# Two attention heads of a pair issued as one interleaved group of half-array matmuls

## The chip, the core and the metric

The kernel runs on one core of a Trainium2 chip. The core has a matrix engine (TensorE, PE in the profile, with its weight loads as a row of their own, PEld), a vector engine (VectorE, DVE), a scalar engine (ScalarE, ACT), GpSimd (POOL) and SyncE (SP), whose queue issues all DMA transfers here. Each engine runs its own list of instructions in order, and they meet at semaphores. TensorE multiplies a stationary operand, loaded into an array of 128 by 128 cells, with a moving operand that streams through it, and writes its sums into eight banks of PSUM. A product with only 64 contraction rows occupies one half of the rows of the array, a product with only 64 stationary columns one half of its columns.

The metric is the device time of one execution in microseconds, as the median of several runs.

## The reference

The reference is two transformer blocks over 256 tokens of width 1024, all in float32. Block 1 has two attentions side by side (latent attention and block attention), and a mixture of 32 experts. Block 2 has an even layer (a gated convolution beside differential attention) and an odd layer (stick-breaking attention), each followed by attention to 256 memory tokens and a gated feed-forward part. Cut to what matters here:

```python
# latent attention: 8 heads, queries and keys 96 wide, values 64 wide
s = jnp.einsum('bqhd,bkhd->bhqk', qi, k) * scale
p = jax.nn.softmax(jnp.where(kpos[None, :] <= qpos[:, None], s, -jnp.inf))
o = jnp.einsum('bhqk,bkhd->bqhd', p, v)
# block attention: 8 heads, all 64 wide; with 256 tokens there is one block, so it is causal attention
# even mixer: 4 pairs of heads, queries and keys 64 wide, values 128 wide
p = probs(q1, k1) - lam * probs(q2, k2);  o = einsum(p, v)
# odd mixer: 16 heads, all 64 wide
z = jnp.einsum('bhqd,bhkd->bhqk', qb, k) * scale
a = exp(log_sigmoid(z) + sum over later keys of log_sigmoid(-z)), keys before the query only
o = jnp.einsum('bhqk,bhkd->bhqd', a, v)
```

## The kernel before

All weights come from memory in slabs of 1 MB. A slab is split into two parts, h on ACT and l on DVE (`slab`, line 539), so that a product with float32 accuracy is made of three products in a faster format, f32r. The helper `fm` (line 658) multiplies a slab with the activations, features by tokens, and `tm` (line 671) tokens by features. Attention itself, the transposes and the statistics are plain float32 matmuls; the profile shows each of those as two passes.

The network is not issued as it is written. Each operation is recorded with the tiles that it reads and writes (`record`, line 223); then a list scheduler (`plan`, line 290) simulates the five engines with a price for each operation (`price`, line 191) and picks an order: on each engine the ready operation that was recorded first goes first, and where none of an earlier phase is ready, one of a later phase does. What is recorded in one call of `record` stays together on its engine; separate calls can come apart. An operation that starts a tile waits for a free place of its tag: `bank` (line 476) gives three banks of PSUM to products with weights, two each to the chains `a` and `b`, to which the pairs of heads go in turn, and one to the rest. The price of a float32 matmul is halved where it uses at most 64 rows or columns. All instructions are issued from line 461, so the profile knows them by their tiles.

Each pair of heads is a chain. In the block attention (`block1_attention`, lines 876 to 892) queries and keys of two heads are transposed together, one head in partitions 0 to 63 and the other in 64 to 127 (tile `qt`). `scores_causal` (line 707) then makes the scores of one head in a bank of its own (`sc`): a 128 by 128 product for the first half of the queries, and a 128 by 256 product for the second half. The mask is added by a bf16 product, DVE takes the maximum (`nm`), ACT the exponential (`p`), and the probabilities are transposed on TensorE and copied to `pt`. `pair_out` (line 917) multiplies them with the values, by `pv` (line 749): two matmuls for each head, 256 and 128 columns, into one half of the partitions of the bank `bo`. When both heads are in, ACT and DVE split the result into `xh` and `xl`.

The latent attention (lines 855 to 869) treats its heads one by one, as they are 96 wide, and uses `pair_out` as well. The even mixer (lines 1352 to 1391) uses `scores_causal` for the two heads of each pair on the tile `eqk`; its value product is 128 wide and is a call of `pv` of its own. The odd mixer (lines 1437 to 1477) makes transposed scores `oz` for both heads of `oqk` in a loop (lines 1450 to 1456), turns them into `op` through `oe`, `oeh` and `oel`, with further products into the same bank, and ends in `pair_out`.

So there are 16 pairs whose scores are 64 rows high (4 in the block attention, 4 in the even mixer, 8 in the odd mixer), and 16 pairs whose values are 64 columns wide (4 in the latent attention, 4 in the block attention, 8 in the odd mixer).

Of the kernel before, what the change touches and what calls it, by code (L numbers as in the profile page):

```python
# [17 lines left out]
PSUM = bass.MemoryType.PSUM  # L18
# [45 lines left out]
# Each engine runs its instructions in the order in which they are issued. The  # L64
# network is first recorded, phase after phase, on tiles that have no place yet;
# a list scheduler then picks the order, so that an engine that would wait for
# one phase works on the next. Tile places the tiles and makes all waits.
class View:
    """A part of a recorded tile."""
# [54 lines left out]
class Slot:  # L124
    """A recorded tile."""
# [38 lines left out]
class Recorder:  # L164
# [18 lines left out]
    def stray(self, shape, dtype, name):  # L183
        """A tile that takes a place that any of the tags in self.shared can spare."""
        return Slot(self, shape, dtype, name, None, 0, "sb").view()
# [97 lines left out]
    def barrier(self, fn, views):  # L283
        """All that was recorded before comes before fn(), all that follows after it, except loads."""
        self.bars.append((len(self.ops), fn, [v.tile for v in views]))
        for v in views:
            v.tile.ops.add(("bar", len(self.bars)))

# [1 line left out]
    def plan(self):  # L290
        """An order of everything recorded: on each engine the ready operation of the lowest prio goes first."""
# [17 lines left out]
        def spare(op):  # L309
            """The shared tag that can best spare a place for op: those of earlier ops stay."""  # L310
            best = None
            for tag in self.shared:
                n = len(free[tag]) - max(0, bisect.bisect_left(self.starts[tag], op.idx) - turn[tag])
                if n > 0 and (best is None or n > best[0]):
                    best = n, tag
            return best and best[1]
# [5 lines left out]
        def load():  # L322
            """Start the loads in the order of the program, as far as there are places."""
            nonlocal due
            while due < len(loads):
                op = loads[due]
                t = op.allocs[0]
                if t.tag is None:
                    tag = spare(op)
                    if tag is None:  # L330
                        return
                    take(op, t, tag)
                elif t.seq == turn[t.tag] and free[t.tag]:
                    take(op, t, t.tag)
                    turn[t.tag] += 1
                else:
                    return
                due += 1
                push(op)
# [4 lines left out]
        def offer(op):  # L344
            """Hand a free place to each tile that op starts, in the order of the program, if there are."""
# [88 lines left out]
    def run(self):  # L434
# [7 lines left out]
        # a table is loaded as soon as the one before has done its last  # L442
# [21 lines left out]
class Net:  # L464
# [11 lines left out]
    def bank(self, tag, name):  # L476
        """A bank of PSUM: g for products with weights, a and b for chains in turn, m for the rest."""
        return self.rec.tile([128, 512], F32, name, "p" + tag, dict(g=3, a=2, b=2, m=1)[tag], "ps")

    def temp(self, p, name, shape, dt=F32):  # L480
        """A short-lived tile of chain p, or of the norms (p = "s")."""
        return self.rec.tile(shape, dt, name, "t" + p, 2 if p == "s" else NT)
# [50 lines left out]
    def raw(self, ap):  # L533
        """A slab of weights as it is."""
        w = self.rec.stray([128, WMAX], F32, "w")
        self.rec.sync.dma_start(w, ap)
        return w

    def slab(self, ap, inner, before=None):
        """A slab of weights in two parts that add up to it exactly, each [128, n / inner, inner].  # L540
        With before, it comes in four pieces, and before(i) comes before piece i."""
# [18 lines left out]
    def mm3(self, todo):  # L560
        """out += s.T @ m, with s = sh + sl and m = mh + ml, for each of todo."""
# [7 lines left out]

    def mm(self, out, lhs, rhs, start=True, stop=True):  # L570
        self.rec.tensor.matmul(out, lhs, rhs, start=start, stop=stop, skip_group_check=True)
# [4 lines left out]
    def parts(self, hi, lo, src, gain=None):  # L576
        """hi + lo = src (times the gain of each partition)."""
# [20 lines left out]
    def rsq(self, p, out, ms, n, mul=1.0):  # L598
        """out = mul / sqrt(ms + EPS), n columns"""
# [11 lines left out]
    def mean(self, acc):  # L611
        """From the sum of squares [128, 2 x 256]: the mean square of each token, on every partition."""
        b = self.bank("m", "st")
        self.rec.vector.tensor_tensor(acc[:, :T], acc[:, :T], acc[:, T:], ALU.add)
        self.mm(b[:, :T], self.k1024, acc[:, :T])
        return b[:, :T]
# [30 lines left out]
    def norm_parts(self, src, gain, stats=True):  # L647
        """Parts of src times gain, and the sum of squares of src."""
# [9 lines left out]
    def fm(self, w, x, kcs=None, cols=0, name="fm", tag="g"):  # L658
        """Two chunks of 128 output features by 256 tokens."""
# [13 lines left out]
    def tm(self, b, w, x, kcs, t, cols, first=True, last=True):  # L673
        """128 tokens by the given columns."""
# [22 lines left out]
    def project(self, w, m):  # L697
        """x += m @ w"""
# [6 lines left out]
    HALVES = ((0, slice(0, 128)), (1, slice(128, 384)))  # L705

    def scores_causal(self, p, q, k):
        """q, k: [d, 256]; scores of both query tiles in one bank: 128 columns of query tile 0, then
        256 of query tile 1."""
# [9 lines left out]
    def softmax_causal(self, p, b, scale=1.0):  # L719
        """exp(scale * (scores - max)) and one over the sums."""  # L720
# [13 lines left out]
    def attend(self, p, b):  # L734
        """Transposed probabilities: key tile 0 by 256 queries, key tile 1 by the last 128."""
# [36 lines left out]
    def block1_attention(self, steps):  # L772
        nc, a = self.rec, self.a
        x, _ = self.norm_parts(self.x, "attn_norm", False)
        # latents of the queries and of the keys and values
# [28 lines left out]
        # by token: rotary key, block attention's queries, keys, values  # L804
# [29 lines left out]
        # latent attention: queries, keys, values by token  # L834
# [41 lines left out]
        for i in range(4):  # L876
            p = "ab"[i % 2]
            bt = self.bank(p, "qkt")
            for n in range(2):
                for t in range(2):  # L880
# [5 lines left out]
            bs = [self.scores_causal(p, qt[64 * j:64 * j + 64, 0:256], qt[64 * j:64 * j + 64, 256:512])  # L886
                  for j in range(2)]
# [5 lines left out]
        # gates  # L893
# [23 lines left out]
    def pair_out(self, p, pts, v, i, ox, c):  # L917
        """Outputs of two heads, from their transposed probabilities."""
        bo = self.bank(p, "bo")
        for j in range(2):  # L920
            hv = slice(128 * i + 64 * j, 128 * i + 64 * j + 64)
            self.pv(bo[64 * j:64 * j + 64, :], v[:, 0, hv], v[:, 1, hv], pts[j])
        self.parts(ox[0][:, c, :], ox[1][:, c, :], bo[:, :T])

# [1 line left out]
    def first_of(self, out, values, best, shape):  # L926
        """One-hot of the first place where values == best."""
# [8 lines left out]
    def route(self, rtm):  # L936
        """Weights and places in line of every token at every expert."""
# [49 lines left out]
        # weights  # L987
# [17 lines left out]
        # those that come after an expert's first SLOTS  # L1005
# [10 lines left out]
    def moe(self, steps, early, every):  # L1016
        nc, a, x = self.rec, self.a, self.x
        # tokens, neither normalised nor times the gain, by token
# [104 lines left out]
    def moe_late(self, hh, hl, rtm, wlate, flag):  # L1123
        """The tokens that come after an expert's first SLOTS, whenever there are any."""
# [64 lines left out]
    def two_norms(self):  # L1189
        """The final norm of block 1 and the first of block 2: parts of x times both gains, and the factor  # L1190
        that normalises their products by token. x becomes the normalised output of block 1."""
# [30 lines left out]
    def head_norm(self, p, b, ones, pairs, rbc, out, gains, mul=1.0):  # L1222
        """Normalise the rows of a bank [128, 2 x 256] by head: over both halves together (pairs)
        or within each (not pairs); out [128, 2, 256]."""
# [18 lines left out]
    def memory(self):  # L1243
        """Keys and values of the memory tokens for both layers, as a list of steps."""
# [84 lines left out]
    def even_mixer(self, x, rbc):  # L1329
# [3 lines left out]
        # lambda  # L1333
# [9 lines left out]
        # distance bias of each head, times 8, with the mask of the last 128 columns  # L1343
# [8 lines left out]
        for hd in range(4):  # L1352
# [10 lines left out]
            bs = []  # L1363
            for m in range(2):
                r = slice(64 * m, 64 * m + 64)
                bs.append(self.scores_causal(p, qk[r, 0, :], qk[r, 1, :]))
# [16 lines left out]
            # sub-layer norm, times 1 - lambda_init  # L1383
# [8 lines left out]
        # gated convolution  # L1392
# [26 lines left out]
    def conv(self, o, u, w):  # L1419
        """Causal convolution of width 3 along the tokens; u has two zero columns in front."""  # L1420
# [5 lines left out]
    def odd_mixer(self):  # L1426
# [10 lines left out]
        for i in range(8):  # L1437
# [12 lines left out]
            bz = []  # L1450
            for j in range(2):
                r = slice(64 * j, 64 * j + 64)
                b = self.bank(p, "oz")
                self.mm(b[:, 0:T], k[r, 0:128], q[r, :], True, False)
                self.mm(b[:, T:384], k[r, 128:T], q[r, 128:T], False, False)
                bz.append(b)
# [106 lines left out]
def layouts(i):  # L1563
    """The inputs as the kernel reads them: moved, never computed on."""
# [119 lines left out]
```

## Time and profile before

| what | value |
|---|---|
| median of 3 runs | 1302.47 us (1300.27 to 1303.06) |
| span of the profiled execution | 1302.4 us |
| TensorE busy | 1234.3 us, 95% |
| DVE busy | 852.8 us, 65% |
| ACT busy | 651.8 us, 50% |
| float32 value products of 64-wide heads (`bo<-pt,vs` and `bo<-op,ov`) | 64 + 64 passes, 28.2 us busy |
| scores of the odd mixer (`oz<-oqk`) | 64 passes, 11.1 us busy |
| scores of the even mixer (`sc<-eqk`) | 32 passes, 3.7 us busy |
| scores in block 1 (`sc<-qt`), latent heads among them | 64 passes, 11.0 us busy |
| DMA | 273.55 MB, mean 210 GB/s |

A row such as `PE MATMUL bo<-op,ov 128*64 128x256 f32 x4` reads: TensorE, operation, the tile written and the tiles read, rows and columns of the array that are used, partitions and elements of the moving operand, and how many such instructions. Matmuls are pipelined and their ends are modelled, so busy time counts overlapping instructions once and says little about what one costs; the distance from one start to the next says more.

### The profile page before, as it was taken

The page shows a single profiled execution, that of the slowest core. Times are in us where ns is not written, and L with a number is a line of the kernel's source. Part 1 is how long each engine was busy: PE and PEld are TensorE (multiplying, and loading weights), DVE is VectorE, ACT ScalarE, POOL GpSimd, SP SyncE. Part 2 cuts the span into 40 slices and gives each one's busy share as a digit, 9 for nine tenths or more (in the row PEclk, how much of TensorE's full clock was granted, in tenths as well). Part 3 has the DMA queues.
Part 4 walks back from the last instruction along what each step waited for, and adds up shares of the span by engine and source line. Part 5 has one row for each costly group of instructions (what it writes and reads, how often), then busy time and mean ns, then how long its engine had stood idle before and what let it go on. Part 6 is the DMA issues. An engine that isn't in the chain of part 4 may idle for free.

```text
span 1302.4 us, 22667 instructions
## 1 busy us (share of the span) xinstructions
PE 1234.3 (95%) x9325; PEld 1091.3 (84%) x9325; DVE 852.8 (65%) x1529; ACT 651.8 (50%) x1111; POOL 8.9 (1%) x71
## 2 busy tenths in 40 slices
PE   7999999987878876999999999999999999999998
PEld 7988999656545542898999999999998999999997
DVE  7666578524442242898877977777745587877775
ACT  6654455423322231664545655555656655555553
POOL 1000000000000000000000000000000000000000
PEclk9999999998989998999999999999999999999999
DMA  7623375798999989353441555555333251555551
GB/s 257 241 98 130 136 285 204 309 393 333 381 379 396 419 335 406 133 191 123 156 175 66 198 196 186 170 191 193 131 130 114 81 194 66 203 185 189 174 188 65
DMA packets 40143, 273.55 MB, mean 210 GB/s; under 512 B 4576, under 2 KB 4576, under 8 KB 8032
## 3 DMA queue, kind: packets, MB, share of 16 engines
q1 hardware_dynamic: 40032, 272.03, 56.1%
q8 instruction: 75, 1.23, 0.4%
q14 instruction: 36, 0.29, 0.1%
HBM read 270.96 MB, written 1.05 MB: 209 GB/s over the span
## 4 chain that ended last, share of the span: by engine, by line
PE 67%; DVE 4%; DMA 2%; ACT 2%; issue 1%; SPq 0%; DVEq 0%; ACTq 0%
PE fm L461 40%; PE dn L461 10%; PE tm L461 4%; PE gu L461 2%; PE co L461 2%; PE oz L461 2%; DMA w<-w_dn 2%; DVE l L461 2%; PE by L461 2%; PE bo L461 1%; PE mo L461 1%; PE ms L461 1%; PE ga L461 1%; PE hn L461 1%; DMA w<-w_gu 1%
## 5 line engine op out<-in xcount | busy, mean ns | idle before, releaser
L461 PE MATMUL fm<-xh,h 128*128 128x256 f32 x1824 | 529.0, 291 | 14.1 <-ACT h L461 6.6
L461 PE MATMUL fm<-xh,l 128*128 128x256 f32 x1824 | 520.1, 286 | 6.7 <-DVE l L461 6.7
L461 PE MATMUL fm<-xl,h 128*128 128x256 f32 x1824 | 518.5, 285 | 0.0
L461 DVE TENSOR_TENSOR l<-w,h 128x1024 fp32r<-128x1024 f32 (+2 forms) x328 | 383.1, 1191 | 59.9 <-ACT h L461 59.2
L461 ACT ACTIVATE h<-w 128x1024 fp32r<-128x1024 f32 (+2 forms) x328 | 325.4, 1027 | 176.3 <-issue 85.1
L461 PEld LDWEIGHTS fm<-xh,h 128*128 128x128 f32 x1824 | 352.0, 193 | 19.2 <-ACT h L461 7.4
L461 PEld LDWEIGHTS fm<-xh,l 128*128 128x128 f32 x1824 | 352.0, 193 | 8.3 <-DVE l L461 8.0
L461 PEld LDWEIGHTS fm<-xl,h 128*128 128x128 f32 x1824 | 352.4, 193 | 2.1 <-issue 0.7
L461 PE MATMUL tm<-l,xh 128*128 128x256 f32 (+2 forms) x364 | 104.5, 288 | 4.0 <-DVE l L461 4.0
L461 PE MATMUL tm<-h,xh 128*128 128x256 f32 (+2 forms) x364 | 107.2, 296 | 0.1
L461 PE MATMUL tm<-h,xl 128*128 128x256 f32 (+2 forms) x364 | 104.0, 286 | 0.0
L461 DVE SCALAR_TENSOR_TENSOR fc<-fu,partile,fc 128x256 f32<-128x256 f32 x176 | 73.5, 480 | 1.3 <-ACT fc L461 1.3
L461 PEld LDWEIGHTS tm<-l,xh 128*128 128x128 f32 x364 | 69.5, 191 | 5.2 <-DVE l L461 4.6
L461 PEld LDWEIGHTS tm<-h,xh 128*128 128x128 f32 x364 | 69.4, 191 | 3.3 <-issue 1.6
L461 PE MATMUL gu<-w,xs 128*32 128x512 f32 x512 | 65.6, 630 | 6.0 <-DMA w<-w_gu 6.0
L461 PEld LDWEIGHTS tm<-h,xl 128*128 128x128 f32 x364 | 69.5, 191 | 0.4
L461 PE MATMUL dn<-fa,h 128*128 128x256 f32 x352 | 64.2, 282 | 1.1 <-ACT fa L461 0.6
L461 DVE TENSOR_TENSOR x<-x,co 128x512 f32<-128x512 f32 x32 | 21.8, 687 | 57.9 <-PE co L461 57.9
L461 PE MATMUL dn<-h,fa 128*128 128x512 f32 x176 | 57.0, 396 | 0.0
L461 PEld LDWEIGHTS dn<-fa,h 128*128 128x128 f32 x352 | 54.4, 189 | 1.6 <-ACT fa L461 0.8
L461 DVE TENSOR_TENSOR fu<-fm,rbc 128x512 f32<-128x512 f32 x44 | 30.3, 688 | 37.9 <-PE fm L461 37.7
L461 DVE SCALAR_TENSOR_TENSOR act<-gu,rs,act 128x256 f32<-128x256 f32 x8 | 3.9, 484 | 71.8 <-ACT act L461 71.8
(291 smaller groups left out, 1416.1 us busy)
## 6 DMA issues: line engine op xcount, KB each, us to landing
w<-w_gu SPq DMA_DIRECT2D x64, 1024.0 KB, 9.3
w<-w_up SPq DMA_DIRECT2D x44, 1024.0 KB, 4.9
w<-w_dn SPq DMA_DIRECT2D x32, 1024.0 KB, 9.9
w<-w_down SPq DMA_DIRECT2D x22, 1024.0 KB, 4.9
w<-w_xkv SPq DMA_DIRECT2D x16, 1024.0 KB, 8.5
w<-w_in_d SPq DMA_DIRECT2D x8, 1024.0 KB, 4.8
w<-w_xq SPq DMA_DIRECT2D x8, 1024.0 KB, 4.9
w<-w_xo SPq DMA_DIRECT2D x8, 1024.0 KB, 5.1
```

Of the source, the lines that this page charges most:

```text
L461: getattr(getattr(self.nc, op.engine), method)(*map(r, a), **{n: r(v) for n, v in k.items()})
```

## The change

Three things become one recorded operation each, in which the two heads take turns: the scores of a pair in the block attention and in the even mixer (new function `scores_pair`), the scores of a pair in the odd mixer, and the value products of a pair in `pair_out`. A new helper `together` records a list of matmuls in one call. In the scores that come from `scores_pair` the 256-wide part now goes first and starts the bank. The latent attention's scores and the even mixer's value product are not touched. Comments and docstrings are gone too, as blank lines, so that most line numbers stay near their old places.

```diff
+    def together(self, *products):
+        self.rec.record("tensor", [("matmul", p[:3], dict(start=p[3], stop=p[4], skip_group_check=True))
+                                   for p in products])
...
+    def scores_pair(self, p, qs, ks):
+        bs = [self.bank(p, "sc") for _ in range(2)]
+        both = list(zip(bs, qs, ks))
+        self.together(*[(b[:, 128:384], q[:, 128:], k, True, False) for b, q, k in both],
+                      *[(b[:, :128], q[:, :128], k[:, :128], False, False) for b, q, k in both])
+        return bs
...
-            bs = [self.scores_causal(p, qt[64 * j:64 * j + 64, 0:256], qt[64 * j:64 * j + 64, 256:512])
-                  for j in range(2)]
+            bs = self.scores_pair(p, *([qt[64 * j:64 * j + 64, o:o + 256] for j in range(2)] for o in (0, 256)))
...
     def pair_out(self, p, pts, v, i, ox, c):
         bo = self.bank(p, "bo")
-        for j in range(2):
-            hv = slice(128 * i + 64 * j, 128 * i + 64 * j + 64)
-            self.pv(bo[64 * j:64 * j + 64, :], v[:, 0, hv], v[:, 1, hv], pts[j])
+        both = [(bo[64 * j:64 * j + 64, :], slice(128 * i + 64 * j, 128 * i + 64 * j + 64), pts[j]) for j in range(2)]
+        self.together(*[(o[:, :T], v[:, 0, hv], pt[:, :T], True, False) for o, hv, pt in both],
+                      *[(o[:, 128:T], v[:, 1, hv], pt[:, T:384], False, True) for o, hv, pt in both])
         self.parts(ox[0][:, c, :], ox[1][:, c, :], bo[:, :T])
...
-            bs = []
-            for m in range(2):
-                r = slice(64 * m, 64 * m + 64)
-                bs.append(self.scores_causal(p, qk[r, 0, :], qk[r, 1, :]))
+            bs = self.scores_pair(p, *([qk[64 * m:64 * m + 64, n, :] for m in range(2)] for n in range(2)))
...
-            bz = []
-            for j in range(2):
-                r = slice(64 * j, 64 * j + 64)
-                b = self.bank(p, "oz")
-                self.mm(b[:, 0:T], k[r, 0:128], q[r, :], True, False)
-                self.mm(b[:, T:384], k[r, 128:T], q[r, 128:T], False, False)
-                bz.append(b)
+            bz = [self.bank(p, "oz") for _ in range(2)]
+            both = [(b, slice(64 * j, 64 * j + 64)) for j, b in enumerate(bz)]
+            self.together(*[(b[:, 0:T], k[r, 0:128], q[r, :], True, False) for b, r in both],
+                          *[(b[:, T:384], k[r, 128:T], q[r, 128:T], False, False) for b, r in both])
```

## The prediction

> **What bounds the kernel now.** I read the page first, then a table of busy time by stretch, then the timeline of TensorE around single heads, and last the waits.
>
> ```profile
> PE 1234.3 (95%) x9325; PEld 1091.3 (84%) x9325; DVE 852.8 (65%) x1529; ACT 651.8 (50%) x1111; POOL 8.9 (1%) x71
> ...
> PE 67%; DVE 4%; DMA 2%; ACT 2%; issue 1%; SPq 0%; DVEq 0%; ACTq 0%
> ```
>
> TensorE is busy for 95% of the span and makes 67% of the chain that ended last. An average hides stages, so the next rows give the stretches that matter (columns: width, then busy time and count on each engine, clock, DMA share, GB/s).
>
> ```profile
> 60.00:112.00 52.00, 52.00 (x394) 45.98 (x394) 30.26 (x70) 28.41 (x68) 0.00 (x0) 1.00 0.34 118
> 112.00:147.00 35.00, 34.88 (x264) 28.83 (x263) 25.87 (x63) 18.91 (x48) 0.00 (x0) 1.00 0.28 97
> 147.00:244.00 97.00, 97.00 (x790) 93.83 (x789) 67.35 (x136) 48.07 (x66) 0.00 (x0) 1.00 0.64 236
> 244.00:520.00 276.00, 223.69 (x1621) 135.92 (x1619) 95.67 (x167) 79.94 (x116) 0.00 (x0) 0.95 0.95 381
> 555.00:625.00 70.00, 67.30 (x520) 62.58 (x519) 64.03 (x146) 38.78 (x81) 0.30 (x3) 0.98 0.43 151
> 915.00:1035.00 120.00, 119.42 (x903) 108.11 (x903) 63.23 (x95) 71.56 (x128) 0.00 (x0) 1.00 0.33 115
> ```
>
> The change touches the latent attention (60 to 112 us), the block attention (112 to 147), the even mixer (555 to 625) and the odd mixer (915 to 1035). In the first two and in the last TensorE has no idle time to speak of, because the planner fills every wait of the attention chains with weight products (`fm`, `tm`). There, time taken from TensorE should be time taken from the kernel. The expert stage between (244 to 520) hangs on DMA, share 0.95.
>
> **What a head's value product costs.** Busy time will not do for this, since matmuls overlap; starts do. The rows are start, length, engine, operation and merged count; a float32 matmul shows as two passes, so one head's two matmuls are x4.
>
> ```profile
> 931.63 0.28 PE L461 MATMUL fm<-xh,l 128*128 128x256 f32 x1
> 931.84 0.87 PE L461 MATMUL bo<-op,ov 128*64 128x256 f32 x4
> 932.64 0.39 PE L461 MATMUL fm<-xh,h 128*128 128x256 f32 x1
> 932.86 0.28 PE L461 MATMUL fm<-xl,h 128*128 128x256 f32 x1
> 932.98 0.28 PE L461 MATMUL fm<-xh,l 128*128 128x256 f32 x1
> ```
>
> In a steady run of `fm` a pass starts every 0.12 us (932.86 to 932.98). From the last `fm` at 931.63 to the second one after the group, at 932.86, 1.23 us pass where two steps would take 0.24: a head standing alone takes 0.99 us of TensorE. Of this 0.80 is the group itself (931.84 to 932.64) and 0.19 the slower entry (0.21 against 0.12) and return (0.22 against 0.12). How many there are:
>
> ```profile
> L461 PE MATMUL bo<-pt,vs 128*64 128x256 f32 (+1 forms) x64 | 14.4, 341 | 0.1
> L461 PE MATMUL bo<-op,ov 128*64 128x256 f32 (+1 forms) x64 | 13.8, 339 | 0.0
> ```
>
> 128 passes are 32 heads, 16 in block 1 and 16 in the odd mixer. The even mixer's value product is 128 wide and stays as it is. In the timeline no two heads' value products stand next to each other, for each is issued when its own probabilities are ready.
>
> **What two heads together cost.** The 64-wide value products exist nowhere side by side in this trace, so their price is bounded. One bound is scores, where two heads use the two row halves:
>
> ```profile
> 924.29 0.93 PE L461 MATMUL oz<-oqk 64*128 64x256 f32 x8
> 925.15 0.40 PE L461 MATMUL oz<-bf 128*128 128x128 bf16 x4
> ...
> 933.54 0.92 PE L461 MATMUL oz<-oqk 64*128 64x256 f32 x4
> 934.39 0.44 PE L461 MATMUL oz<-oeh,ntri 128*128 128x384 f32 x1
> 934.76 0.92 PE L461 MATMUL oz<-oqk 64*128 64x256 f32 x4
> 935.61 0.40 PE L461 MATMUL oz<-bf 128*128 128x128 bf16 x4
> ```
>
> Eight passes of two neighbouring heads take 0.86 us to the next operation, four passes of one head 0.85: the second head costs 0.01 us if it is next in the queue. This also says that adjacency alone is enough here, since the code before records all of one head and then all of the other. The interleaved order itself should be worth nothing. The other near row is the expert product, 32 columns wide, four column parts at once:
>
> ```profile
> 393.81 7.07 PE L461 MATMUL gu<-w,xs 128*32 128x512 f32 x64
> ...
> 394.27 0.13 PEld L461 LDWEIGHTS gu<-w,xs 128*32 128x32 f32 x4 [0.30 <-issue]
> ```
>
> 64 passes of 512 columns in 7.07 us are 0.11 us a pass, 0.22 ns a column; a lone head streams 768 columns in 0.80 us, 1.04 ns a column. So column parts run side by side as well, and four of their weight loads fit in 0.13 us. The other bound is no overlap at all: the second head then adds its whole 0.80. I take 0.01, the value of the row case, because the column row shows the same kind of overlap in the very direction that is asked of here.
>
> So a pair of value products goes from 2 x 0.99 to 1.00, and saves 0.97 us; 16 pairs save **15.6 us**. With no overlap it would be 0.19 a pair, 3.0 us.
>
> **What the scores save.** Where both heads already stand together nothing is left to gain: all four pairs of the even mixer (one is quoted), three of four in the block attention and two of eight in the odd mixer.
>
> ```profile
> 561.17 0.93 PE L461 MATMUL sc<-eqk 64*128 64x128 f32 x8
> 562.03 0.50 PE L461 MATMUL sc<-ali,bf 128*128 128x128 bf16 x4
> ```
>
> ```profile
> 126.08 0.92 PE L461 MATMUL sc<-qt 64*128 64x128 f32 x4
> 129.04 0.92 PE L461 MATMUL sc<-qt 64*128 64x128 f32 x4
> ```
>
> ```profile
> 958.75 0.92 PE L461 MATMUL oz<-oqk 64*128 64x256 f32 x6
> 959.60 0.86 PE L461 MATMUL bo<-op,ov 128*64 128x256 f32 x4
> 960.39 0.48 PE L461 MATMUL oz<-oqk 64*128 64x128 f32 x2
> 960.81 0.40 PE L461 MATMUL oz<-bf 128*128 128x128 bf16 x4
> ```
>
> ```profile
> 975.24 0.70 PE L461 MATMUL oz<-oqk 64*128 64x256 f32 x2
> 975.86 0.44 PE L461 MATMUL oz<-oel,ntri 128*128 128x384 f32 x1
> 976.45 0.92 PE L461 MATMUL oz<-oqk 64*128 64x128 f32 x6
> 977.31 0.40 PE L461 MATMUL oz<-bf 128*128 128x128 bf16 x4
> ```
>
> The pair at 126.08 and 129.04, and that at 933.54 and 934.76, are fully apart: about 0.97 each (0.85 and a switch). The kind at 958.75, three times in the odd mixer, takes 0.85 + 0.42 against 0.86 together and saves 0.41 and half a switch, 0.5 each. The kind at 975.24, twice, takes 0.62 + 0.86 against 0.86 and saves 0.62 and half a switch, 0.7 each. Together 1.0 in block 1 and 1.0 + 1.5 + 1.4 = 3.9 in the odd mixer, **4.9 us**. Starting the bank with the 256-wide part instead of the 128-wide one costs nothing: 924.29 and 561.17 have the two orders, and both take 0.86.
>
> **What is added and moved.** No DMA, no copy and no instruction is new. The first head's value product is moved behind the second head's probabilities. The group then waits for both on TensorE, and behind it in that queue stand the `fm` passes of the next slab, for whose banks DVE waits. But the second head's product waits for the same thing today, and that has cost almost nothing:
>
> ```profile
> PE bo L461 <- DVE pt L461: 0.3, 1, 0.3
> ```
>
> The output bank is evacuated when the second head is done, in both versions. Scores must now find two free banks of their chain at once; in the even mixer they find them at every pair, so I cost this at nothing. The cover is the stock of `fm` passes; what it costs without it is the third rival.
>
> One term comes back. In the block attention DVE is busy for 25.87 of 35 us; with about 4.9 us less TensorE (4 x 0.97 + 1.0) it would be 86%. In the even mixer, where DVE has 64.03 of 70 us (91%), TensorE idles 2.7 us, 3.9%. By that row the 30 us left would hold 1.2 us of new idle time.
>
> **Sum.** 15.6 + 4.9 - 1.2 = 19.3 us. The profiled span is 1302.4 us, 0.1 from the median of the runs (1302.47), so 1302.4 - 19.3 = **1283**.
>
> **Rivals.**
>
> First, the two column halves do not overlap. Then 3.0 + 4.9 - 0.5 (a smaller DVE term) leave about 1295. For it: no 64-wide pair is in the trace. Against it: the expert rows above. The Trainium skill has a rule that speaks for it: "TensorE: Matmul & The Clock Gate", Part 3, says that weight loads overlap running matmuls only where the row group differs, and two value products use the same rows. By that rule, each head's loads and passes would follow one another, and the kernel would end near the time of this rival; the four `gu` loads within 0.13 us, all on the same rows, disagree with it. Chance 8%.
>
> Second, what is gained in block 1 is swallowed by the expert stage, whose loads then start no earlier. Lost would be 8 x 0.97 + 1.0 - 1.2 = 7.6 us, leaving about 1291. For it: the DMA share of 0.95. Against it: before that stage the share is 0.64, and the queue is held by buffers that the engines free:
>
> ```profile
> SPq L461 <- DVE l L461: 62.8, 11, 8.3
> ```
>
> This is the waits of the DMA queue from 147 to 244 us: eleven waits for slabs to be split, which come sooner if TensorE does. Chance 13%.
>
> Third, slower: the joined groups tie the heads of a pair, the planner runs out of `fm` passes at the end of the block attention and of the odd mixer, and the last chain of each lies bare.
>
> ```profile
> 137.23 0.39 ACT L461 ACTIVATE xh<-bo 128x256 fp32r<-128x256 f32 x1 [1.18 <-PE bo L461]
> ...
> 994.86 0.37 ACT L461 ACTIVATE xh<-bo 128x256 fp32r<-128x256 f32 x1
> ```
>
> A chain takes 11.2 us from scores to evacuation there (126.08 to 137.23) and 19.6 here (975.24 to 994.86). Both bare cost 30.8 against 20.5 saved: about 1313. It decides once new idle time of TensorE passes 20.5 us. Against it: the idle time in these stretches is now 0.1 and 0.6 us, and the end of a chain is set by its second head, which moves nowhere. Chance 6%. Fourth, the same mechanism or a poorer order elsewhere gives back just what is gained: about 1302, 5%.
>
> **Chances and range.** The forecast has 68%. Less than 0.2%, 2.6 us, can't be told from no change. Faster: the forecast and the first two rivals, 0.89, less a little for their tails, 0.88; same 0.05; slower 0.07. The forecast's own range is 1278 (no DVE term, and a list order that happens to need fewer switches) to 1289; down to 1275 for a luckier order and up to 1296 it takes in the first two rivals.
>
> **What would show it.** Right: `bo` of block 1 and the odd mixer in runs of x8 that last 0.8 to 0.9 us to the next operation; `oz` always x8; TensorE still without idle time from 60 to 147 us and in the odd mixer, which is some 11 us shorter; the even mixer unchanged; the expert stage as long as before, but some 7 us earlier. Wrong: `bo` x8 of 1.5 us or more (first rival), the first loads of the experts at the old time (second), or idle rows before `bo` and `fm` at the stage ends (third).

## The result and the profile after

The changed kernel takes 1282.09 us (median of 4 runs, 1278.79 to 1284.22) against 1302.69 us (4 runs): 0.9845 of the time, 95% interval 0.9826 to 0.9865, or 20.6 us less. The forecast was 1283. In a second comparison the same kernel took 1283.3 us against 1301.18, 0.9862 (0.9836 to 0.9888).

The page of the changed kernel has the same shape as before: TensorE at 95%, and 67% of the chain that ended last.

```profile
PE 1207.3 (95%) x9325; PEld 1078.8 (84%) x9325; DVE 851.4 (67%) x1529; ACT 649.5 (51%) x1111; POOL 8.9 (1%) x71
...
PE 67%; DVE 4%; DMA 2%; ACT 2%; issue 1%; SPq 0%; DVEq 0%; ACTq 0%
```

The table of busy time by stretch, for both attentions of block 1, the block attention alone, the time from there to the experts, the even mixer and the odd mixer (columns as in the prediction):

```profile
59.70:137.20 77.50, 77.47 (x648) 70.90 (x646) 53.63 (x130) 45.68 (x113) 0.00 (x0) 1.00 0.34 122
105.50:138.00 32.50, 32.47 (x283) 29.24 (x282) 25.42 (x63) 19.71 (x50) 0.00 (x0) 1.00 0.33 118
138.00:235.00 97.00, 97.00 (x792) 93.66 (x795) 68.16 (x138) 48.23 (x66) 0.00 (x0) 1.00 0.65 237
542.00:610.00 68.00, 65.27 (x516) 61.23 (x515) 63.31 (x145) 38.66 (x81) 0.30 (x3) 1.00 0.43 153
910.10:1004.80 94.70, 94.70 (x794) 88.91 (x794) 51.21 (x76) 61.76 (x116) 0.00 (x0) 1.00 0.36 126
```

TensorE is still without idle time in the attentions (77.47 busy of 77.50 us) and in the odd mixer, so the time went out of TensorE's own work. The timeline shows where. A pair of value products in the odd mixer, to be held against the lone head at 931.84 in the prediction:

```profile
922.89 0.28 PE L461 MATMUL fm<-xh,l 128*128 128x256 f32 x1
923.11 0.87 PE L461 MATMUL bo<-op,ov 128*64 128x256 f32 x8
923.91 0.39 PE L461 MATMUL fm<-xh,h 128*128 128x256 f32 x1
924.13 0.28 PE L461 MATMUL fm<-xl,h 128*128 128x256 f32 x1
```

Eight passes now take 0.80 us to the next operation, as four did before, and the way from the last `fm` to the second one after the group is 1.24 us against 1.23. The second head is all but free. A pair of scores with the value products of another pair behind it:

```profile
932.42 0.92 PE L461 MATMUL oz<-oqk 64*128 64x256 f32 x8
933.27 0.87 PE L461 MATMUL bo<-op,ov 128*64 128x256 f32 x8
934.07 0.40 PE L461 MATMUL oz<-bf 128*128 128x128 bf16 x4
```

Before, the value product of a single head could come between the scores of a pair and cut them in two (958.75 to 960.39 in the prediction). In this profile all eight groups of `oz` are x8 and take 0.85 or 0.86 us, and of the 16 groups of value products 14 take 0.80 or 0.81 us; the other two are in the latent attention and come up further below.

For the stages I use the rows of single tiles: each has the shortest, median and longest instruction in ns, then the first and the last start in us. Before:

```profile
L461 PE MATMUL qkt<-csttile,qm x16: 270/272/313, 61.2 to 92.7; 128*96 128x128 f32 x16
L461 PE MATMUL bo<-pt,vs x64: 272/351/431, 74.4 to 146.0; 128*64 128x256 f32 x32, 128*64 128x128 f32 x32
L461 PE MATMUL xt<-csttile,x x16: 270/273/328, 221.5 to 227.1; 128*128 128x128 f32 x16
L461 PE MATMUL co<-cs,y x128: 379/379/796, 258.3 to 527.9; 128*128 128x256 f32 x128
L461 PE MATMUL oz<-oqk x64: 269/374/480, 924.3 to 1014.5; 64*128 64x256 f32 x32, 64*128 64x128 f32 x32
L461 PE MATMUL bo<-op,ov x64: 272/326/431, 931.8 to 1029.4; 128*64 128x256 f32 x32, 128*64 128x128 f32 x32
```

After:

```profile
L461 PE MATMUL qkt<-csttile,qm x16: 270/272/313, 59.7 to 88.8; 128*96 128x128 f32 x16
L461 PE MATMUL bo<-pt,vs x64: 272/351/431, 74.7 to 137.2; 128*64 128x256 f32 x32, 128*64 128x128 f32 x32
L461 PE MATMUL xt<-csttile,x x16: 270/273/328, 212.0 to 217.6; 128*128 128x128 f32 x16
L461 PE MATMUL co<-cs,y x128: 379/379/483, 250.0 to 515.2; 128*128 128x256 f32 x128
L461 PE MATMUL oz<-oqk x64: 269/324/480, 910.1 to 990.8; 64*128 64x256 f32 x32, 64*128 64x128 f32 x32
L461 PE MATMUL bo<-op,ov x64: 272/326/430, 923.1 to 1004.0; 128*64 128x256 f32 x32, 128*64 128x128 f32 x32
```

From these rows, and the same rows of every other run, comes this table (us, between starts): the attentions of block 1 from the first `qkt` to the last `bo<-pt,vs`, then on to the first `xt` (the experts' first transposes), the experts to the last `co`, the even mixer from the first `sc<-eqk` to the last `bo<-pt,ev`, and the odd mixer from the first `oz<-oqk` to the last `bo<-op,ov`.

| profiled run | attentions of block 1 | on to `xt` | experts | even mixer | odd mixer |
|---|---|---|---|---|---|
| before | 84.8 | 75.5 | 306.3 | 57.2 | 105.1 |
| the change | 77.4 | 74.8 | 303.2 | 55.7 | 93.8 |
| the change, second profile | 77.4 | 74.8 | 304.3 | 55.7 | 93.8 |
| values only | 77.6 | 75.5 | 310.8 | 57.2 | 94.3 |
| scores only | 85.4 | 74.8 | 307.4 | 57.2 | 101.5 |
| joined, head by head | 77.3 | 74.8 | 303.8 | 55.7 | 93.9 |
| joined, same column half | 81.4 | 75.6 | 307.2 | 57.2 | 100.1 |
| block 1 only | 77.4 | 74.8 | 304.3 | 55.7 | 105.2 |
| odd mixer only | 84.8 | 75.5 | 308.0 | 55.7 | 93.8 |

Block 1 gives 7.4 and 0.7 us, the odd mixer 11.3. That is 19.4 us. The profiled execution of the changed kernel is the shortest of its four: its span of 1277.0 us lies 25.4 under that of before, and the other 6.0 are, but for rounding, 1.5 at the start (first `qkt` at 59.7 instead of 61.2), 3.1 in the experts and 1.5 in the even mixer. The even mixer differs by as much between the kernel before and the one with the odd mixer alone (57.2 and 55.7), whose programs are the same up to there, so this does not hang on the change. For the experts it is less clear: the four profiles with all of block 1 joined in opposite halves have 303.2 to 304.3 us, the five others 306.3 to 310.8. With one profile for each program, whether a part of these 3 us belongs to the change is not shown.

### The profile page after: what moved, and what is told of

The parts are those of the page before. It is cut to its first block, busy times and chain, and to the rows that moved or that the text cites. A ratio compares the mean times of both kernels' runs of the same rounds, so it can differ in the third digit from the quotient of the medians.

```text
span 1277.0 us, 22671 instructions
## 1 busy us (share of the span) xinstructions
PE 1207.3 (95%) x9325; PEld 1078.8 (84%) x9325; DVE 851.4 (67%) x1529; ACT 649.5 (51%) x1111; POOL 8.9 (1%) x71
## 3 DMA queue, kind: packets, MB, share of 16 engines
q8 instruction: 75, 1.23, 0.4%
## 4 chain that ended last, share of the span: by engine, by line
PE 67%; DVE 4%; DMA 2%; ACT 2%; issue 1%; SPq 0%; DVEq 0%; ACTq 0%
PE fm L461 41%; PE dn L461 10%; PE tm L461 4%; PE gu L461 2%; DMA w<-w_dn 2%; PE co L461 2%; DVE l L461 2%; PE oz L461 1%; PE by L461 1%; PE mo L461 1%; PE ms L461 1%; PE ga L461 1%; PE hn L461 1%; DMA w<-w_gu 1%; PE bo L461 1%
```

## The experiments

Each diff here is against the changed kernel. The theory: two heads in two halves of the array cost as much as one, whatever order they stand in, so long as they are next to each other in TensorE's queue; that is worth 15.6 us in the value products and 4.9 us in the scores, and it goes straight through to the end. The rivals: the halves of columns do not overlap; it is fewer groups and waits, not overlap, that bring the gain; and what block 1 gains is lost in the expert stage.

### The value products alone

The scores go back to their separate calls, the value products stay joined.

```diff
-            bs = self.scores_pair(p, *([qt[64 * j:64 * j + 64, o:o + 256] for j in range(2)] for o in (0, 256)))
+            bs = [self.scores_causal(p, qt[64 * j:64 * j + 64, 0:256], qt[64 * j:64 * j + 64, 256:512])
+                  for j in range(2)]
...
(in the same way for the even mixer and the odd mixer)
```

> Only the value products are joined; the scores are recorded head by head as before. Theory (16 pairs of value products save 0.97 us each, less 1.2 for DVE): the terms of the values alone give 1302.5 - 14.4 = 1288. But the planner's order for this kernel, which can be seen before it runs, already has six of the eight odd pairs and all but one of the others with their scores next to each other: if adjacency is all that counts, most of the 4.9 us of the scores come along, and the time is 1283 to 1286. Rival (it is the joined scores that bring the gain): 1298 or more.

Measured: 1283.93 us against 1303.32 (0.9849, 0.9817 to 0.988). The odd mixer takes 94.3 us instead of 93.8, and the attentions of block 1 77.6 instead of 77.4. One pair of scores in the odd mixer is still cut by a value group, at 943.90:

```profile
943.90 0.92 PE L461 MATMUL oz<-oqk 64*128 64x256 f32 x6
944.75 0.87 PE L461 MATMUL bo<-op,ov 128*64 128x256 f32 x8
945.55 0.49 PE L461 MATMUL oz<-oqk 64*128 64x128 f32 x2
945.96 0.40 PE L461 MATMUL oz<-bf 128*128 128x128 bf16 x4
```

All seven others of the odd mixer stand side by side without having been joined, one more than the expectation had counted; in the block attention one pair of four is cut. By the table this kernel is 1.4 us longer than the change (0.2 + 0.7 + 0.5), which the runs can't tell apart. So joining the value products brings nearly the whole gain, and most of the scores' share comes with it. That the planner has less to put between the scores once the values are joined is the likely reason; it was not tested by itself.

### The scores alone

```diff
     def pair_out(self, p, pts, v, i, ox, c):
         bo = self.bank(p, "bo")
-        both = [(bo[64 * j:64 * j + 64, :], slice(128 * i + 64 * j, 128 * i + 64 * j + 64), pts[j]) for j in range(2)]
-        self.together(...)
+        for j in range(2):
+            hv = slice(128 * i + 64 * j, 128 * i + 64 * j + 64)
+            self.pv(bo[64 * j:64 * j + 64, :], v[:, 0, hv], v[:, 1, hv], pts[j])
```

> Only the scores are joined; value products go head by head as before. Theory: 4.9 us from the scores (1.0 in the block attention, 3.9 in the odd mixer, 0 in the even mixer), so 1297.6, and oz in eight groups of x8 of 0.86 us. Rival (the scores are the larger part): 1290 or less.

Measured: 0.9974 of the time before, with an interval of 0.9951 to 0.9997, so 3.4 us less (0.4 to 6.4). Joining the scores is the smaller part of the gain. The odd mixer is 3.6 us shorter, where 3.9 were reckoned, and its `oz` are eight groups of x8, as expected. But the attentions of block 1 are 0.6 us longer and the time from there to `xt` 0.7 shorter: together 0.1 us gained, where 1.0 was reckoned. The timeline there shows the value product of a head split by transposes, as it already was for three of the latent heads:

```profile
127.94 0.65 PE L461 MATMUL bo<-pt,vs 128*64 128x256 f32 x2
128.51 0.33 PE L461 MATMUL pt<-csttile,p 128*128 128x128 f32 x1
128.77 0.43 PE L461 MATMUL bo<-pt,vs 128*64 128x128 f32 x2
129.13 0.44 PE L461 MATMUL pt<-csttile,p 128*128 128x128 f32 x2
129.50 0.92 PE L461 MATMUL sc<-qt 64*128 64x256 f32 x8
```

The scores are together (x8 at 129.50), and a value product that was whole in this stage before is in two parts. The split alone costs some 0.3 us (0.57 + 0.36 against 0.80, and one more entry); what the rest of the missing 0.9 is made of was not followed further.

### Joined, but head by head

Everything joined as in the change, with all of the first head ahead of all of the second. For the value products:

```diff
-        self.together(*[(o[:, :T], v[:, 0, hv], pt[:, :T], True, False) for o, hv, pt in both],
-                      *[(o[:, 128:T], v[:, 1, hv], pt[:, T:384], False, True) for o, hv, pt in both])
+        self.together(*[t for o, hv, pt in both for t in ((o[:, :T], v[:, 0, hv], pt[:, :T], True, False),
+                                                          (o[:, 128:T], v[:, 1, hv], pt[:, T:384], False, True))])
```

> All groups joined as in the change, but within a group all of the first head comes before all of the second. Theory (being next in the queue is enough, the order of turns is worth nothing): the time of the change, 1282, and value groups of x8 of 0.80 us. Rival (the column halves overlap only if the heads take turns): value groups of about 1.4 to 1.6 us, 16 x 0.7 = 11 us more, 1293.

Measured: 1283.3 us (0.9853, 0.9822 to 0.9884), the time of the change. A value group of this kernel:

```profile
925.85 0.28 PE L461 MATMUL fm<-xh,l 128*128 128x256 f32 x1
926.06 0.88 PE L461 MATMUL bo<-op,ov 128*64 128x256 f32 x8
926.87 0.38 PE L461 MATMUL fm<-xh,h 128*128 128x256 f32 x1
```

0.81 us, with the first head's second matmul ahead of the second head's first one in the program. The order of turns is worth nothing here; being adjacent is enough. The Trainium skill, in "TensorE: Matmul & The Clock Gate", Part 3, says that matmuls start strictly in the order of the program. By that rule the second head could not start before the first head's second matmul, which starts 0.48 us into the group in this trace, and its own passes, 0.64 us by the next experiment (1.44 less 0.80), would then bring the group above 1.1; the 0.81 us do not agree with it. Nor do the starts: the second head's first pass is 0.01 us behind that of the first head (926.07 and 926.06), ahead of the first head's second matmul.

### Joined, but in the same half

Both heads are sent through the same 64 columns, into two ranges of the bank in partitions 0 to 63, and ACT moves each to its partitions afterwards.

```diff
-        both = [(bo[64 * j:64 * j + 64, :], slice(128 * i + 64 * j, 128 * i + 64 * j + 64), pts[j]) for j in range(2)]
+        both = [(bo[:64, T * j:T * j + T], slice(128 * i + 64 * j, 128 * i + 64 * j + 64), pts[j]) for j in range(2)]
-        self.together(*[(o[:, :T], v[:, 0, hv], pt[:, :T], True, False) for o, hv, pt in both],
+        self.together(*[(o, v[:, 0, hv], pt[:, :T], j == 0, False) for j, (o, hv, pt) in enumerate(both)],
...
-        self.parts(ox[0][:, c, :], ox[1][:, c, :], bo[:, :T])
+        bc = self.temp("s", "bc", [128, T])
+        for j in range(2):
+            self.rec.scalar.activation(bc[64 * j:64 * j + 64, :], both[j][0], AF.Copy)
+        self.parts(ox[0][:, c, :], ox[1][:, c, :], bc)
```

> Joined as in the change, but both heads of a pair of value products use the same column half of the array (two column ranges of the bank in partitions 0 to 63), so that they can't overlap; ACT then copies each head to its partitions, 32 more ACT copies of about 0.4 us off TensorE's path. Scores as in the change. Theory (the gain is the overlap of two halves): value groups of 1.4 to 1.6 us, a pair takes 1.8 instead of 1.0, 3.0 + 4.9 = 8 us less than before, about 1294. Rival (the gain comes from fewer groups and waits, not from overlap): 1282 to 1284.

Measured: 1294.65 us (0.9933, 0.9907 to 0.9959).

```profile
933.71 0.28 PE L461 MATMUL fm<-xh,l 128*128 128x256 f32 x1
933.92 1.51 PE L461 MATMUL bo<-op,ov 128*64 128x256 f32 x8
935.36 0.39 PE L461 MATMUL fm<-xh,h 128*128 128x256 f32 x1
```

The same eight passes now take 1.44 us instead of 0.80. Over 16 pairs that is 10.2 us, and the table shows 4.0 + 0.8 + 6.3 = 11.1 us between this kernel and the change. So of the 19.4 us that the table gives the change, some 11 hang on the overlap of the value products; the rival is right only in what is left, since attentions and odd mixer are still 3.4 and 5.0 us shorter than before the change, by the joined scores and the switches saved. What is beyond the 10.2 us, 0.9, can be the added ACT copies or another order; that is open.

### One block at a time

The change in block 1 alone, and in the odd mixer alone. `pair_out` has both forms:

```diff
-    def pair_out(self, p, pts, v, i, ox, c):
+    def pair_out(self, p, pts, v, i, ox, c, joined):
...
-            self.pair_out(p, es, v, i, ox, i)
+            self.pair_out(p, es, v, i, ox, i, False)
```

The diff is that of block 1 alone; the other kernel has True here and False at the two calls in block 1. The scores follow suit.

> The change in block 1 alone (value products of the latent and the block attention, scores of the block attention); both mixers of block 2 as before. Theory (what block 1 gains passes through the expert stage): the stretch of the two attentions 77.4 us instead of 84.8, and the whole kernel 7 to 8 us faster than before, 1295. Rival (the expert stage, which hangs on DMA, swallows it): the stretch is as short, but the kernel takes 1302 and the stage from the first transposes of the experts to its last product is 7 us longer.

> The change in the odd mixer alone (its scores and value products). Theory: first score to last value product 94 us instead of 105, the kernel 11 to 12 us faster than before, 1291. Under the rival of the expert stage this kernel would be as fast as the whole change, 1282.

> The change itself once more, beside the two halves on the same chip. Theory: 1282 to 1284, and its gain is the sum of the gains of the two halves, 7.4 + 11.3 = 18.7 us, within the 3 us that the medians can tell.

Measured on the same chip: block 1 alone 0.9930 (0.9907 to 0.9953), the odd mixer alone 0.9920 (0.9892 to 0.9948), both 0.9862 (0.9836 to 0.9888). By these ratios the three are 9.1, 10.4 and 18.0 us below 1301.18, and their intervals reach 3 to 4 us to either side; the halves add up to 19.5. By the medians (1293.32, 1292.77 and 1283.3) it is 7.9, 8.4 and 17.9. Within that the gains add up. In block 1 alone the attentions run from 60.8 to 138.2 and the odd mixer from 912.2 to 1017.3:

```profile
L461 PE MATMUL qkt<-csttile,qm x16: 270/272/313, 60.8 to 89.8; 128*96 128x128 f32 x16
L461 PE MATMUL bo<-pt,vs x64: 272/351/431, 75.7 to 138.2; 128*64 128x256 f32 x32, 128*64 128x128 f32 x32
L461 PE MATMUL bo<-op,ov x64: 272/326/431, 919.8 to 1017.3; 128*64 128x256 f32 x32, 128*64 128x128 f32 x32
L461 PE MATMUL oz<-oqk x64: 269/374/480, 912.2 to 1002.5; 64*128 64x256 f32 x32, 64*128 64x128 f32 x32
```

What block 1 gains reaches the end: its experts take 304.3 us, not more than before (306.3), and start earlier, and the interval of the whole kernel's time (0.9907 to 0.9953) lies clear of no gain. The rival of the expert stage falls.

## Why the prediction was right

**The price of a joined pair** was the step on which most hung, and it had been bounded only from both sides. The value taken, 0.01 us for the second head, is what the trace shows (0.80 for eight passes and for four). The other end, no overlap, is the kernel with both heads in the same half; there the second head adds 0.64 us (1.44 less 0.80), not its whole 0.80, so this end of the bound was set too high. The rival drawn from the Trainium skill ("TensorE: Matmul & The Clock Gate", Part 3: weight loads overlap running matmuls only where the row group differs) falls with it, for these pairs use the same rows and overlap in full.

**The scores** had their sizes right in the odd mixer (3.6 measured alone, 3.9 reckoned). For the block attention the 1.0 was not seen when they were joined alone. And the two terms do not simply add: in the odd mixer the values alone give 10.8 us and the scores alone 3.6, together 11.3. The prediction put the sum at 7.8 + 3.9 = 11.7 and came out close, but its term for the values alone was 7.8, where they brought 10.8: in the kernel with the values alone, seven of eight pairs of scores stand together too. Two slips in the prediction's sums hardly matter: 2 x 0.99 less 1.00 is 0.98, not 0.97, and 0.85 with a switch of 0.19 is 1.04, not 0.97.

**The term for DVE** was wrong in kind. The prediction gave back 1.2 us in the block attention, because DVE would be the tighter engine. TensorE has 0.03 us of idle time there (32.50 and 32.47), and DVE is at 78% of the stretch, not 86%. The row of the even mixer could not bear the term: 2.07 of its 2.7 us of idle time are a single wait at the end of the stage (the row at 610.18 in the last section), not a loss spread over the stage that could be carried to another one. Block 1 gave 8.1 us where the prediction has 8.8 before this term is taken off, so 0.7 went elsewhere, and the agreement of the whole sum is in part luck. A loss of that size is seen in the latent attention: two of its four value pairs overlap only in part.

```profile
80.94 0.65 PE L461 MATMUL bo<-pt,vs 128*64 128x256 f32 x2
81.52 0.39 PE L461 MATMUL tm<-h,xh 128*128 128x256 f32 x1
81.83 0.86 PE L461 MATMUL bo<-pt,vs 128*64 128x256 f32 x6
82.63 0.42 PE L461 MATMUL qkt<-csttile,qm 128*96 128x128 f32 x2
...
91.92 1.07 PE L461 MATMUL bo<-pt,vs 128*64 128x256 f32 x8
92.92 0.39 PE L461 MATMUL tm<-h,xh 128*128 128x256 f32 x1
```

DVE's timeline has the copies of the second heads' probabilities:

```profile
80.97 0.55 DVE L461 COPY pt<-pt 128x384 f32<-128x384 f32 x1
...
91.52 0.56 DVE L461 COPY pt<-pt 128x384 f32<-128x384 f32 x1 [0.82 <-PE pt L461]
```

They end at 81.52 and 92.08, after the first head has started (80.94 and 91.92). The first pair takes 1.69 us with a `tm` pass of 0.12 between, 0.77 too much, the second 1.00, 0.20 too much: 1.0 us together. The `tm` pass also shows that a group recorded in one call does not always stay in one piece in TensorE's queue. It is not what stops the overlap: in the kernel with one head after the other the same pair is whole and takes 1.43 us.

```profile
83.42 1.50 PE L461 MATMUL bo<-pt,vs 128*64 128x256 f32 x8
84.85 0.42 PE L461 MATMUL qkt<-csttile,qm 128*96 128x128 f32 x2
```

The prediction had said that the second head's wait is the same as today and costs nothing. TensorE indeed does not idle, but a head that starts late runs beside nothing, and so the wait is paid in lost overlap.

**The second rival**, block 1 swallowed by the experts, is answered above. The waits of the DMA queue between the attentions and the experts (137 to 235 us) are of the kind that was seen before, for the slabs that the engines release:

```profile
SPq L461 <- DVE l L461: 61.9, 11, 8.3
```

**The third rival**, chains laid bare at the stage ends, did not come: in the odd mixer TensorE is busy for all of 94.70 us, and from the end of the block attention on for all of 97.00.

**The stages as forecast**: the odd mixer 11.3 us shorter (some 11), block 1 7.4 and 0.7 (7.6). The even mixer was to be unchanged and is 1.5 us shorter in this profile, but not through the change: it is as short in the kernel with block 1 alone, whose even mixer is that of before, and as long as before in three kernels whose scores or values are joined. Where it is long, TensorE's clock is what differs, as the last section shows.

## What to carry to other kernels

Here the float32 products of two heads in opposite halves of the array cost as much as those of one when they are neighbours in TensorE's queue, in either order (0.80 us in column halves, 0.86 in row halves). A scheduler that issues each as soon as it is ready separates them, and then each pays in full, with a switch on both sides. Find such pairs by the distance from the start of a group to the next start, not by busy time, and tie them into one unit. Tie them where the later of the two is ready in time, because the one that runs first and alone loses the overlap although nothing waits.

## What had not been expected of the hardware

A plain float32 group of 64 columns between f32r products costs TensorE more than its passes: 0.21 us in and 0.22 out, where a step is 0.12. It was read from the trace beforehand, yet its weight surprised: some 0.19 us for each such group that the change does away with. What in the switch takes the time is open.

The granted clock fell in the middle of this single-core kernel after a pause of TensorE of 2.07 us. In the profile of before, the pause and the busy time by 5 us at the end of the even mixer:

```profile
610.18 0.39 PE L461 MATMUL fm<-xh,h 128*128 128x256 f32 x1 [2.07 <-DVE cu L461]
...
605.00:610.00 5.00, 3.11 (x28) 2.42 (x26) 4.12 (x14) 2.64 (x8) 0.09 (x1) 1.00 0.47 192
610.00:615.00 5.00, 4.82 (x27) 4.82 (x28) 5.00 (x14) 2.69 (x9) 0.01 (x1) 0.66 0.02 3
```

TensorE is busy for 3.11 of 5 us, and in the next 5 us the clock is 0.66. In the changed kernel's profile it is 1.00 over the whole even mixer, with the same pause:

```profile
597.53 0.39 PE L461 MATMUL fm<-xh,h 128*128 128x256 f32 x1 [2.07 <-DVE cu L461]
```

All nine profiles have this pause, 2.06 to 2.08 us long; in four of them the clock falls behind it, and those are the four whose even mixer takes 57.2 us instead of 55.7. So a pause of this length meets the drop in some executions and not in others. The experts, 303.2 to 310.8 us, vary more than that, for reasons that were not followed, while the attentions of the change and its odd mixer repeat within 0.1 us. A single profiled span, 25.4 us shorter here, says less than the lengths of the stages that the change touches.
